# Forgetting attention: last keys in an idle ring, head 0's loads ahead of a store, later heads' loads tied to the release of their tiles

## The chip, the cores and the metric

The kernel runs on one core of one Trainium2 chip. Its engines are TensorE (PE in the profile; PEld is its weight load), VectorE (DVE), ScalarE (ACT), GpSimd (POOL) and SyncE (SP), which only issues transfers. The metric is the device time of one execution in microseconds. All data are float32; a float32 product is made of three matmuls over a high and a low part of each operand.

## The reference, cut to what matters

The reference is one residual block over 1024 tokens of width 1024: a norm, one projection into three token mixers, their merge with sigmoid gates, an output projection, and a gated feed-forward part. The change touches the second mixer, forgetting attention, with 8 heads of width 64:

```python
qh = _rmsnorm(q.reshape(B, T, FOX_HEADS, FOX_DH), q_g).transpose(0, 2, 1, 3)
kh = _rmsnorm(k.reshape(B, T, FOX_HEADS, FOX_DH), k_g).transpose(0, 2, 1, 3)
log_f = jax.nn.log_sigmoid(f_logit + f_bias)
Fc = jnp.cumsum(log_f, axis=1).transpose(0, 2, 1)
for blk in range(T // Q_BLOCK):                    # 8 blocks of 128 queries
    lo, hi = blk * Q_BLOCK, (blk + 1) * Q_BLOCK
    s = (jnp.einsum('bhqd,bhkd->bhqk', qh[:, :, lo:hi], kh[:, :, :hi]) * scale
         + Fc[:, :, lo:hi, None] - Fc[:, :, None, :hi])
    p = jax.nn.softmax(jnp.where(mask, s, -jnp.inf), axis=-1)
    outs.append(jnp.einsum('bhqk,bhkd->bhqd', p, vh[:, :, :hi]))
```

The first mixer is a gated recurrence; its decay needs the logarithm and the running sum of a projected gate, per head.

## The kernel before, in words

The program is written in stages, and a list scheduler, which works on estimated durations, sets the order of the instructions on each engine. Priorities (`high_priority`) and `issue_after` (this instruction is not placed ahead of that one) steer it. On the chip each engine then runs its own list strictly in order and waits by semaphores. SP's transfers use eight semaphores in turn, so each issue also waits until the transfer eight places ahead has landed.

**Projections with tokens as rows** (`stage`, `tm_unit`). The last of these stages, `stage(4, put_fqk(1))`, makes the normed keys and queries of heads 4 to 7. `put_fqk` appends two steps, `keys(0)` and `keys(1)`, for each quarter of the product: four transposes on TensorE into PSUM, a cast to the high part on ACT (line 628), the low part on DVE (line 629), both into a tile `ko`, and one SP store of 512 KB into the DRAM tensor `kqd` of the head pair (line 639). `ko` is a ring of two tiles, so a cast has to await the landing of the store two before. The ring `ws` beside it, of two tiles as large, holds sums of weights in these stages. The last quarter is c = 1, n = 0 of head pairs 2 and 3.

**The fill** (`fill_steps`, `cm_unit`). The remaining projections, for the recurrence and the gates, are units of seven products of Strassen's kind; their matmuls are the rows with `pp<-B11h,uh`, `T2h`, `T3h` and so on. A unit loads four tiles `ur` of weights (SP, line 802), makes sums `us` on POOL, casts `uh` on ACT, the remainder `ul` on DVE. A result goes into a tile `uo` (a ring of two) and to the DRAM tensor `hgd` of its head of the recurrence, from SP (line 789) or, for the gate, from POOL (line 782). In between, `decays(h)` loads the stored gate into one tile `fk` (SP, line 950), works on it on DVE (953, 954), takes its logarithm on ACT (956), scans (959, 960), and stores it.

**The attention** (`fox_attn`, woven with the fill head by head, and ahead of it in priority). `fox_load` fetches for a head: `kh`, `qa`, `kl`, each in two halves of 256 KB, one pair of tiles for even heads and one for odd; the cumulated gate `nf`, 2 x 256 KB; the values `vhl`, 512 KB. Lines 1030 and 1031 are the logits, first qa with kh, then qa with kl, into a PSUM ring `lg` of two. DVE adds the bias and takes the maximum (line 1036; the diagonal's bias `nfm` comes from POOL), ACT exponentiates (1046), POOL divides (1048), TensorE transposes (1059 to 1062) and multiplies with the values into the single PSUM bank `po` (1071, 1072). `yp` (ACT copy 1075, DVE sum 1076) empties that bank, and SP stores it into `yd` (1077), four stores a head. In this kernel the loads of every head but the first are tied to `marks["head"]`, the first of the four `yd` stores of the head before. The tiles of the attention lie where the rings `ko`, `ws` and others of the projections lay, and await their release.

Of the kernel before, what the change touches and what calls it, by code (L numbers as in the profile page):

```python
# [9 lines left out]
F32 = mybir.dt.float32  # L10
F32R = mybir.dt.float32r
# [4 lines left out]
P = 128  # L16
# [3 lines left out]
HB = 512  # L20
# [13 lines left out]
AHEAD = 300  # L34
# [35 lines left out]
def tile_block(ctx: ExitStack, tc: tile.TileContext, xT, x_rows, memT, vec, fbias, mats, hmask, w_ff, w_tm, w_cm,  # L70
               w_mkv, w_br, w_out, w_up, w_dn, outT):
    nc = tc.nc
    V, S, G, PE, SP = nc.vector, nc.scalar, nc.gpsimd, nc.tensor, nc.sync
# [33 lines left out]
    def col(i):  # L107
        return cv[:, i:i + 1]
# [47 lines left out]
    negFd = tc.dram_tile([8, T], F32, name="negFd")  # L156
    kqd = [tc.dram_tile([2, P, 2, T], F32, name=f"kqd{p}") for p in range(4)]
    vhd = [tc.dram_tile([P, 8, 4, P], F32, name=f"vhd{c}") for c in range(2)]
# [20 lines left out]
    def ws_tile(name="ws", dt=F32):  # L179
        return rp.tile([P, T], dt, tag="ws", name=name, bufs=2)  # L180
# [7 lines left out]
    def ko_tile(name="ko", dt=F32R):  # L188
        return rp.tile([P, 2, HB], dt, tag="ko", name=name, bufs=2)
# [430 lines left out]
    def turned(z, what, gc, tiles, ptr):  # L620

        for b in range(4):
            PE.transpose(ptr[:, b * P:(b + 1) * P], z[:, b, what * P:(what + 1) * P], ident)
        h, l = tiles
        if gc is None:
            split(S, h, l, ptr)
            return
        S.activation(h, ptr, AF.Copy, scale=gc)
        V.scalar_tensor_tensor(out=l, in0=ptr, scalar=gc, in1=h.bitcast(F32), op0=ALU.mult, op1=ALU.subtract)

    def put_fqk(pp):
        def put(c, n, z, bank):
            p = 2 * pp + c
            head_norm(z, 4, bank)

            def keys(what):
                t = ko_tile()
                turned(z, what, col(C_FK) if what == 0 else fqs, (t[:, 0, :], t[:, 1, :]), bank[what])
                SP.dma_start(kqd[p][what][:, :, n * HB:(n + 1) * HB], t.bitcast(F32))
            pending.append(lambda: keys(0))  # L640
            pending.append(lambda: keys(1))
        return put
# [89 lines left out]
    marks = {}  # L732
# [27 lines left out]
    def put_gate(i):  # L760
# [7 lines left out]
            S.dma_start(gd[i, n], t)  # L768
        return put

    def put_hg(what, h):
        def put(c, n, ps, e):
            t = out_tile()
            dst = hgd[h][what][:, n * HB:(n + 1) * HB]
            if what == 0:
                if e is None:
                    S.activation(t, ps, AF.Tanh, scale=-0.5)
                else:
                    combine(t, ps, e, c)
                    S.activation(t, t, AF.Tanh, scale=0.5)  # L780
                G.tensor_scalar(t, t, TMIN, TMAX, ALU.max, ALU.min)
                G.dma_start(dst, t)
                return
            else:
                z = e if e is not None else ur.tile([P, HB], F32, tag="ue", name="ue", bufs=3)
                combine(z, ps, e, c)
                S.activation(t, z, AF.Tanh, scale=0.5)
                V.scalar_tensor_tensor(out=t, in0=t, scalar=1.0, in1=z, op0=ALU.add, op1=ALU.mult)
            SP.dma_start(dst, t)
        return put  # L790

    def cm_unit(u, puts):
# [197 lines left out]
    resets = pf.tile([P, 256], F32, tag="resets", name="resets")  # L990
    SP.dma_start(resets, mats[:, 3 * P:3 * P + 256])
    mskf = pf.tile([P, P], F32, tag="mskf", name="mskf")
    with tc.high_priority(2 * AHEAD):
        SP.dma_start(mskf, mats[:, 2 * P:3 * P])

    def fox_load(h):
        p, a = h // 2, slice(64 * (h % 2), 64 * (h % 2) + 64)
        kh, qa, kl = (pf.tile([P, T], F32R, tag=f"{t}{h % 2}", name=f"{t}_{h}") for t in ("kh", "qa", "kl"))
        for t, (u, v) in ((kh, (0, 0)), (qa, (2, 3)), (kl, (1, 1))):
            SP.dma_start(t[0:64, :].bitcast(F32), kqd[p][u // 2][a, u % 2, :])  # L1000
            SP.dma_start(t[64:128, :].bitcast(F32), kqd[p][v // 2][a, v % 2, :])
        nf = [pf.tile([P, HB], F32, tag="nf", name="nf", bufs=3) for _ in range(2)]
        for n, t in enumerate(nf):
            SP.dma_start(t, negFd[h:h + 1, n * HB:(n + 1) * HB].partition_broadcast(P))
        vhl = pf.tile([P, 8, P], F32R, tag="vhl", name="vhl", bufs=2)
        SP.dma_start(vhl.bitcast(F32), vhd[h // 4][:, :, h % 4, :])
        return kh, kl, qa, vhl, nf

    begun = marks["product"]

    def fox_attn(h):
        p, a = h // 2, slice(64 * (h % 2), 64 * (h % 2) + 64)
        with tc.issue_after(marks["head"].ins) if h else nullcontext():
            kh, kl, qa, vhl, nf = fox_load(h)
        for tp in range(4):
            pts = []
            for j in range(2):
# [59 lines left out]
            stored = SP.dma_start(yd3[1][a, p, tp * 256:(tp + 1) * 256], yp)  # L1077
            if tp == 0:
                marks["head"] = stored
            yield  # L1080

    for h in range(8):
# [479 lines left out]
    for p in range(NF // 2):  # L1562
# [41 lines left out]
        for i in range(2):  # L1604
            f = 2 * p + i
            c = pq.tile([P, T], F32, tag="fc", name="fc", bufs=4)
# [89 lines left out]
    for a, b, own, first, c, n, sign, last, xq in (  # L1696
# [6 lines left out]
        dst = banks if own else ybanks  # L1703
# [130 lines left out]
```

## Time and profile before

| what | value |
|---|---|
| median of 3 runs (lowest, highest) | 1690.49 us (1685.17, 1690.71) |
| the profiled execution | 1690.35 us, its span 1688.6 us |
| attention heads in the span | first logits at 333.6 us, first logits of kh in the last head up to 669.7 us |
| TensorE busy | 98% of the span |
| DVE, ACT, POOL busy | 72%, 50%, 27% |

A row of a timeline has the start in us, the duration, the engine, the line, the operation with output and inputs, the shapes, a count where equal ones were merged, and in brackets the idle time of that engine just before, with what ended it. Rows of SPq are issues of transfers; their duration is that of the issue. A group of transfers ends with the size and the us from issue to landing.

### The profile page before, as it was taken

To read this page: it belongs to the slowest core of one execution; us is meant where nothing else is said; L and a number is where in the kernel's file an instruction comes from. 1 tells how busy PE (TensorE), PEld (TensorE's weight loads), DVE (VectorE), ACT (ScalarE), POOL (GpSimd) and SP (SyncE) were. 2 spreads that over 40 slices of the span, in tenths; PEclk is the share of its full clock that TensorE was granted. 3 is DMA by queue.
4 is the path that set the end of the run, shared out by engine and by line. 5 is a ranking of instruction groups with operands and counts; after the bars stand their busy time and mean duration, and the time that the engine had idled before them with its cause. 6 is when DMAs were issued, how large, how long until landed. Compare 5 with 4: busy or idle time off the path is not lost. (4 is left out here: it accounts for less than half of the span.)

```text
span 1688.6 us, 24989 instructions
## 1 busy us (share of the span) xinstructions
PE 1658.2 (98%) x8915; PEld 1419.6 (84%) x8915; DVE 1218.8 (72%) x2173; ACT 845.8 (50%) x1453; POOL 449.7 (27%) x475
## 2 busy tenths in 40 slices
PE   8999999999899999999999999899999999999999
PEld 6989999787788888888888788788888888888887
DVE  6775766588776766688766768877887878675664
ACT  7645554466666666556333267534444443343432
POOL 0143543556554444223001053311111110100000
PEclk9999999999999999999999999999999999999999
DMA  7352443565455552647866798856543452394782
GB/s 268 109 188 90 142 166 119 186 203 162 159 159 156 153 160 95 200 132 231 314 185 163 246 225 209 235 164 183 166 131 119 138 158 81 127 392 154 240 281 88
DMA packets 132637, 298.73 MB, mean 177 GB/s; under 512 B 14072, under 2 KB 31736, under 8 KB 131872
## 3 DMA queue, kind: packets, MB, share of 16 engines
q1 hardware_dynamic: 100864, 210.08, 36.8%
q0 software_dynamic: 22432, 72.36, 16.6%
q10 hardware_dynamic: 9216, 14.68, 2.3%
q8 instruction: 70, 1.15, 0.3%
q14 instruction: 55, 0.45, 0.1%
HBM read 216.40 MB, written 103.22 MB: 189 GB/s over the span
## 5 line engine op out<-in xcount | busy, mean ns | idle before, releaser
L1349 ACT CAST wh<-s 128x512 fp32r<-128x512 f32 x80 | 49.0, 620 | 118.9 <-PE pp L123 66.2
L128 ACT CAST dwh<-wr 128x1024 fp32r<-128x1024 f32 (+1 forms) x41 | 40.2, 981 | 114.9 <-PE tr L123 39.3
L1487 POOL DMA_DIRECT2D rw<-in_w_up x40 | 22.9, 602 | 244.4 <-DVE wl L1350 175.7
L1349 ACT CAST wh<-rw 128x512 fp32r<-128x512 f32 x70 | 42.8, 620 | 85.3 <-PE pp L123 43.3
L736 ACT CAST uh<-ur 128x512 fp32r<-128x512 f32 x78 | 48.2, 618 | 70.7 <-PE pp L123 67.4
L737 DVE TENSOR_TENSOR ul<-us,uh 128x512 fp32r<-128x512 f32 x72 | 55.2, 771 | 21.5 <-ACT uh L736 21.4
L1048 POOL TENSOR_SCALAR pt<-pt,st 128x128 f32<-128x128 f32 (+3 forms) x64 | 56.6, 885 | 52.5 <-DVE st L1047 32.8
L1046 ACT ACTIVATE pt<-pt,st 128x128 f32<-128x128 f32 (+3 forms) x64 | 49.8, 778 | 41.1 <-DVE st L1043 35.8
L136 DVE TENSOR_TENSOR dwl<-wr,dwh 128x1024 fp32r<-128x1024 f32 (+1 forms) x41 | 46.3, 1130 | 31.8 <-ACT dwh L128 31.7
L122 PE MATMUL pp<-B21h,uh 128*128 128x512 f32 x168 | 66.7, 399 | 2.2 <-DVE ue L150 1.2
L123 PE MATMUL pp<-T2l,uh 128*128 128x512 f32 x168 | 67.0, 399 | 0.0
L122 PE MATMUL pp<-T2h,uh 128*128 128x512 f32 x168 | 66.8, 401 | 0.0
L737 DVE TENSOR_TENSOR ul<-ur,uh 128x512 fp32r<-128x512 f32 x78 | 61.9, 795 | 6.5 <-ACT uh L736 6.0
L742 POOL TENSOR_TENSOR us<-ur 128x512 f32<-128x512 f32 x36 | 50.7, 1408 | 59.3 <-DMA ur<-in_w_cm 43.8
L124 PE MATMUL pp<-B21h,ul 128*128 128x512 f32 x168 | 66.2, 394 | 0.1
L124 PE MATMUL pp<-T2h,ul 128*128 128x512 f32 x168 | 66.2, 395 | 0.0
L123 PE MATMUL pp<-B21l,uh 128*128 128x512 f32 x168 | 66.0, 393 | 0.0
L736 ACT CAST uh<-us 128x512 fp32r<-128x512 f32 x72 | 43.9, 615 | 38.3 <-POOL us L742 21.9
L1350 DVE TENSOR_TENSOR wl<-rw,wh 128x512 fp32r<-128x512 f32 x70 | 47.0, 686 | 18.9 <-PE pp L124 15.3
L742 POOL TENSOR_TENSOR us<-us,ur 128x512 f32<-128x512 f32 x36 | 49.5, 1375 | 39.4 <-issue 33.8
L1024 POOL TENSOR_TENSOR nfm<-nf,mskf 128x128 f32<-128x128 f32 x64 | 37.9, 592 | 77.5 <-DVE st L1036 56.1
L136 DVE TENSOR_TENSOR wl<-raw,wh 128x1024 fp32r<-128x1024 f32 x29 | 38.1, 1323 | 25.6 <-ACT wh L128 25.3
(746 smaller groups left out, 6188.7 us busy)
## 6 DMA issues: line engine op xcount, KB each, us to landing
rw<-in_w_up POOLq DMA_DIRECT2D x40, 512.0 KB, 4.8
ur<-in_w_cm SPq DMA_DIRECT2D x72, 256.0 KB, 3.3
sd<-in_w_dn POOLq DMA_DIRECT2D x30, 512.0 KB, 8.3
br<-yd SPq DMA_DIRECT2D x30, 512.0 KB, 5.5
gd<-uo ACTq DMA_DIRECT2D x48, 256.0 KB, 3.1
gt<-gd SPq DMA_DIRECT2D x48, 256.0 KB, 4.5
yd<-fc SPq DMA_DIRECT2D x44, 256.0 KB, 2.8
raw<-in_w_tm SPq DMA_DIRECT2D x20, 512.0 KB, 3.5
```

The costliest lines, as they stand in the source:

```text
L122: PE.matmul(ps, lh, rh, start=first, stop=False, skip_group_check=more)
L123: PE.matmul(ps, lh, rl, start=False, stop=False, skip_group_check=more)
L124: return PE.matmul(ps, ll, rh, start=False, stop=last, skip_group_check=more)
L128: S.copy(out, in_)
L136: return (sub or V).tensor_sub(l, src, h.bitcast(F32))
L736: marks["cast"] = S.copy(h, src)
L737: V.tensor_sub(l, src, h.bitcast(F32))
L742: G.tensor_add(t, a, b)
L1046: S.activation(pt[:, :ns], pt[:, :ns], AF.Exp, bias=st[:, 2:3], accum_out=st[:, 3:4])
L1048: G.tensor_scalar(pt[:, :ns], pt[:, :ns], st[:, 3:4], 0.0, ALU.mult, ALU.add)
L1349: late["cast"] = S.copy(h, src)
L1350: late["split"] = V.tensor_sub(l, src, h.bitcast(F32))
```

## The change

1. The last two key tiles (pair 3, second half; written `(pp, c, n) == (1, 1, 0)`) are taken from the ring `ws` and no longer from `ko`.
2. The store of the second half of the query gate q of the recurrence's head 0 (`put_hg(1, 0)`, n = 1) is held back and issued only behind head 0's six key and query loads; these get the higher priority, with the mask `mskf` that had it alone.
3. Head 1's six loads are tied to that store, those of head h from 2 on to the last `yd` store of head h - 2, whose tiles they reuse. `nf` stays behind the first `yd` store of the head before, `vhl` goes behind the six loads.

```diff
             def keys(what):
                 t = ko_tile()
+                if (pp, c, n) == (1, 1, 0):
+                    t = ws_tile("ko", F32R).rearrange("p (a b) -> p a b", a=2)
...
-            SP.dma_start(dst, t)
+            if (what, h, n) == (1, 0, 1):
+                put_late.append(partial(SP.dma_start, dst, t))
+            else:
+                marks["stored"] = SP.dma_start(dst, t)
...
-    with tc.high_priority(2 * AHEAD):
-        SP.dma_start(mskf, mats[:, 2 * P:3 * P])
...
-        for t, (u, v) in ((kh, (0, 0)), (qa, (2, 3)), (kl, (1, 1))):
-            SP.dma_start(t[0:64, :].bitcast(F32), kqd[p][u // 2][a, u % 2, :])
-            SP.dma_start(t[64:128, :].bitcast(F32), kqd[p][v // 2][a, v % 2, :])
+        before = ends.get(h - 2) or marks["stored"] if h else None
+        with tc.issue_after(before.ins) if before else tc.high_priority(2 * AHEAD):
+            for t, (u, v) in ((kh, (0, 0)), (qa, (2, 3)), (kl, (1, 1))):
+                SP.dma_start(t[0:64, :].bitcast(F32), kqd[p][u // 2][a, u % 2, :])
+                loaded = SP.dma_start(t[64:128, :].bitcast(F32), kqd[p][v // 2][a, v % 2, :])
+        if not h:
+            with tc.high_priority(2 * AHEAD):
+                SP.dma_start(mskf, mats[:, 2 * P:3 * P])
+            with tc.issue_after(loaded.ins):
+                marks["stored"] = put_late.pop()()
         nf = [pf.tile([P, HB], F32, tag="nf", name="nf", bufs=3) for _ in range(2)]
-        for n, t in enumerate(nf):
-            SP.dma_start(t, negFd[h:h + 1, n * HB:(n + 1) * HB].partition_broadcast(P))
+        with tc.issue_after(marks["head"].ins) if h else nullcontext():
+            for n, t in enumerate(nf):
+                SP.dma_start(t, negFd[h:h + 1, n * HB:(n + 1) * HB].partition_broadcast(P))
         vhl = pf.tile([P, 8, P], F32R, tag="vhl", name="vhl", bufs=2)
-        SP.dma_start(vhl.bitcast(F32), vhd[h // 4][:, :, h % 4, :])
+        with tc.issue_after(loaded.ins):
+            SP.dma_start(vhl.bitcast(F32), vhd[h // 4][:, :, h % 4, :])
...
-        with tc.issue_after(marks["head"].ins) if h else nullcontext():
-            kh, kl, qa, vhl, nf = fox_load(h)
+        kh, kl, qa, vhl, nf = fox_load(h)
...
+            ends[h] = stored
```

Since the scheduler starts over with these ties, the order moves on all engines from here to the middle of the merge of the branches. Three places of it follow. Line numbers of the changed kernel are 2 to 15 higher: 1006 and 1007 are its loads of kh, qa and kl, 1012 the store held back, 809 ur, 1044 and 1045 the logits.

First, SP between the last key stores and head 0's loads, before:

```order
L639 DMA kqd_96<-ko 256x1x512
L802 DMA ur<-in_w_cm 128x512
L639 DMA kqd_96<-ko 256x1x512
L789 DMA hgd_101<-uo 128x512
L994 DMA mskf<-in_mats 128x128
L1000 DMA kh_3815<-kqd_93 64x1024
L1001 DMA kh_3815<-kqd_93 64x1024
L1000 DMA qa_3816<-kqd_93 64x1024
L1001 DMA qa_3816<-kqd_93 64x1024
L1000 DMA kl_3817<-kqd_93 64x1024
L1001 DMA kl_3817<-kqd_93 64x1024
```

and now, on to head 1's loads (kh_4151, qa_4152):

```order
L641 DMA kqd_96<-ko 256x1x512 x2
L809 DMA ur<-in_w_cm 128x512
L1006 DMA kh_3815<-kqd_93 64x1024
L1010 DMA mskf<-in_mats 128x128
L1007 DMA kh_3815<-kqd_93 64x1024
L1006 DMA qa_3816<-kqd_93 64x1024
L1007 DMA qa_3816<-kqd_93 64x1024
L1006 DMA kl_3817<-kqd_93 64x1024
L1007 DMA kl_3817<-kqd_93 64x1024
L1012 DMA hgd_101<-uo 128x512
```

```order
L796 DMA hgd_101<-uo 128x512
L1006 DMA kh_4151<-kqd_93 64x1024
L1007 DMA kh_4151<-kqd_93 64x1024
L1006 DMA qa_4152<-kqd_93 64x1024
L1007 DMA qa_4152<-kqd_93 64x1024
L1006 DMA kl_4153<-kqd_93 64x1024
L1007 DMA kl_4153<-kqd_93 64x1024
L1019 DMA vhl<-vhd_97 128x8x128
L796 DMA hgd_101<-uo 128x512
L957 DMA fk_4262<-hgd_101 128x1024
L809 DMA ur<-in_w_cm 128x512 x4
```

The two last key stores moved together, the fill's store of hgd moved behind head 0's loads, and seven loads of head 1 moved ahead of the decay's load and the next unit's weights.

Second, TensorE around the low part of head 0's first two logits, before:

```order
L122 MATMUL pp<-T2h,uh 128x512
L123 MATMUL pp<-T2l,uh 128x512
L124 MATMUL pp<-T2h,ul 128x512
L124 MATMUL pp<-T1h,ul 128x512
L1031 MATMUL lg<-kl_3817,qa_3816 128x128
L1031 MATMUL lg<-kl_3817,qa_3816 128x256
```

and now:

```order
L1044 MATMUL lg<-kh_3815,qa_3816 128x128
L1044 MATMUL lg<-kh_3815,qa_3816 128x256
L1045 MATMUL lg<-kl_3817,qa_3816 128x128
L1045 MATMUL lg<-kl_3817,qa_3816 128x256
L122 MATMUL pp<-T1h,uh 128x512
L123 MATMUL pp<-T1l,uh 128x512
```

The products with kl moved up past 15 matmuls of the fill, to right behind those with kh.

Third, DVE at the decays' tile of the recurrence's last head (fk_6499 before, fk_6501 now; before, a `yp` stood right behind it), before:

```order
L1036 ISA pt,st<-lg,nf 128x512
L1036 ISA st 128x1
L953 TENSOR_SCALAR fk_6499<-fk_6499,nc_71,c1p 128x1024
L1076 TENSOR_TENSOR yp<-po,yp 64x256
L1036 ISA pt,st<-lg,nf 128x128
```

and now, where that `yp` stands 19 rows ahead:

```order
L739 TENSOR_TENSOR ul<-ur,uh 128x512
L1055 TENSOR_TENSOR st<-st 128x1
L960 TENSOR_SCALAR fk_6501<-fk_6501,nc_71,c1p 128x1024
L1057 TENSOR_SCALAR st<-st 128x1
L961 TENSOR_SCALAR fk_6501<-fk_6501,c_70,c_69 128x1024
L1090 TENSOR_TENSOR yp<-po,yp 64x256
L148 SCALAR_TENSOR_TENSOR ue<-pp,ue 128x512
```

The first decay operation moved behind one `yp` and now has the next `yp` three rows behind it.

More of the change, by code (lines that the diff above doesn't have):

```diff
@@ L769, in put_gate @@
         return put
+    put_late = []
     def put_hg(what, h):
@@ L998, in fox_load @@
         kh, qa, kl = (pf.tile([P, T], F32R, tag=f"{t}{h % 2}", name=f"{t}_{h}") for t in ("kh", "qa", "kl"))
-        for t, (u, v) in ((kh, (0, 0)), (qa, (2, 3)), (kl, (1, 1))):
-            SP.dma_start(t[0:64, :].bitcast(F32), kqd[p][u // 2][a, u % 2, :])
-            SP.dma_start(t[64:128, :].bitcast(F32), kqd[p][v // 2][a, v % 2, :])
+        before = ends.get(h - 2) or marks["stored"] if h else None
[8 more added lines that the diff above has]
+                marks["stored"] = put_late.pop()()
         nf = [pf.tile([P, HB], F32, tag="nf", name="nf", bufs=3) for _ in range(2)]
-        for n, t in enumerate(nf):
-            SP.dma_start(t, negFd[h:h + 1, n * HB:(n + 1) * HB].partition_broadcast(P))
+        with tc.issue_after(marks["head"].ins) if h else nullcontext():
+            for n, t in enumerate(nf):
+                SP.dma_start(t, negFd[h:h + 1, n * HB:(n + 1) * HB].partition_broadcast(P))
         vhl = pf.tile([P, 8, P], F32R, tag="vhl", name="vhl", bufs=2)
-        SP.dma_start(vhl.bitcast(F32), vhd[h // 4][:, :, h % 4, :])
+        with tc.issue_after(loaded.ins):
+            SP.dma_start(vhl.bitcast(F32), vhd[h // 4][:, :, h % 4, :])
         return kh, kl, qa, vhl, nf
+    ends = {}
     begun = marks["product"]
```

## The prediction, made before the changed kernel ran

> **What bounds the kernel now.** I read the page first, for the share of TensorE, then the same busy times by stretches of the run, to see where TensorE is not busy.
>
> ```profile
> span 1688.6 us, 24989 instructions
> PE 1658.2 (98%) x8915; PEld 1419.6 (84%) x8915; DVE 1218.8 (72%) x2173; ACT 845.8 (50%) x1453; POOL 449.7 (27%) x475
> ...
> 300.00:400.00 100.00, 94.08 (x470) 77.07 (x469) 72.45 (x173) 59.06 (x106) 59.60 (x52) 0.98 0.59 195
> 400.00:420.00 20.00, 19.32 (x102) 16.17 (x101) 17.85 (x53) 11.90 (x24) 9.56 (x10) 1.00 0.55 144
> 420.00:440.00 20.00, 17.33 (x97) 14.83 (x97) 14.30 (x34) 13.56 (x23) 8.67 (x9) 1.00 0.57 201
> 440.00:460.00 20.00, 18.35 (x95) 15.20 (x94) 14.26 (x39) 11.90 (x24) 13.52 (x15) 1.00 0.38 127
> 600.00:700.00 100.00, 100.00 (x534) 85.36 (x534) 64.00 (x173) 59.01 (x118) 38.17 (x44) 1.00 0.37 117
> ```
>
> After a stretch and its length, such a row has the busy time of PE, PEld, DVE, ACT and POOL, then the granted TensorE clock, the DMA share and GB/s. TensorE bounds the kernel. Only 1688.6 - 1658.2 = 30.4 us of the span are idle on it, and 5.92 + 0.68 + 2.67 + 1.65 = 10.9 us of these lie between 300 and 460 us, where heads 0 to 2 of the forgetting attention run; in the last heads, from 600 to 700, it is full. The change can take off no matmul. It can win idle time and slow-clock time in that stretch, and lose some anywhere up to the gated sums.
>
> Next the clock in steps of 5 us, and TensorE's own waits in order of time:
>
> ```profile
> 330.00:335.00 5.00, 2.58 (x12) 1.84 (x11) 1.19 (x2) 0.17 (x1) 2.70 (x3) 0.93 1.01 246
> 335.00:340.00 5.00, 5.00 (x19) 4.05 (x18) 1.97 (x7) 2.24 (x4) 0.76 (x2) 0.73 1.13 354
> 435.00:440.00 5.00, 5.00 (x31) 4.38 (x30) 4.99 (x10) 2.71 (x4) 1.00 (x1) 1.00 0.72 261
> 460.00:465.00 5.00, 5.00 (x21) 4.12 (x20) 5.00 (x15) 4.44 (x4) 1.52 (x1) 0.66 0.89 230
> ...
> 333.61 0.47 PE L1030 MATMUL lg<-kh,qa 128*128 128x128 f32 x2 [2.42 <-DMA qa<-kqd]
> 333.92 0.40 PE L122 MATMUL pp<-T1h,uh 128*128 128x512 f32 x1
> 338.95 0.39 PE L1031 MATMUL lg<-kl,qa 128*128 128x128 f32 x2
> 351.35 0.39 PE L122 MATMUL pp<-B11h,uh 128*128 128x512 f32 x1
> 371.04 0.30 PE L1031 MATMUL lg<-kl,qa 128*128 128x128 f32 x1 [1.10 <-DMA kl<-kqd]
> 419.73 0.30 PE L1031 MATMUL lg<-kl,qa 128*128 128x128 f32 x1 [0.68 <-DMA kl<-kqd]
> 434.65 0.36 PE L1071 MATMUL po<-ph,vhl 128*128 128x256 f32 x1 [2.67 <-DVE yp L1076]
> 458.91 0.36 PE L1071 MATMUL po<-ph,vhl 128*128 128x256 f32 x1 [1.59 <-DVE yp L1076]
> ```
>
> Head 0's first logits wait 2.42 us for its loads, and the clock is low just behind: 5 x (0.07 + 0.27) = 1.7 us. The wait of 1.59 us at 458.91 is followed by 5 x 0.34 = 1.7 us of the same; that of 2.67 us at 434.65 is not. Of the waits, those of 2.42, 1.10 and 0.68 are ended by a head's loads, those of 2.67 and 1.59 by DVE.
>
> [...]
>
> **Part 1: the last keys and head 0's loads.** SP, ACT and DVE ahead of the first logits, and landing times of those transfers:
>
> ```profile
> 314.17 1.28 DVE L737 TENSOR_TENSOR ul<-us,uh 128x512 fp32r<-128x512 f32 x2
> 317.00 0.69 ACT L628 ACTIVATE ko<-lg,cv 128x512 fp32r<-128x512 f32 x1 [2.84 <-PE pp L124]
> 317.72 0.75 DVE L629 SCALAR_TENSOR_TENSOR ko<-lg,cv,ko 128x512 fp32r<-128x512 f32 x1 [2.28 <-ACT ko L628]
> 321.05 0.69 ACT L628 ACTIVATE ko<-lg,fqs 128x512 fp32r<-128x512 f32 x1 [2.36 <-DMA kqd<-ko]
> 315.60 0.64 SPq L802 DMA_DIRECT2D ur<-in_w_cm  x1
> 322.55 0.52 SPq L639 DMA_DIRECT2D kqd<-ko  x1
> 325.39 0.52 SPq L1000 DMA_DIRECT2D kh<-kqd  x1
> 327.58 0.45 SPq L1001 DMA_DIRECT2D qa<-kqd  x1
> 328.73 0.58 SPq L1001 DMA_DIRECT2D kl<-kqd  x1
> ...
> kqd<-ko SPq DMA_DIRECT2D x1, 512.0 KB, 4.9
> kqd<-ko SPq DMA_DIRECT2D x1, 512.0 KB, 6.1
> qa<-kqd SPq DMA_DIRECT2D x1, 256.0 KB, 5.9
> hgd<-uo POOLq DMA_DIRECT2D x1, 256.0 KB, 7.2
> DMA to landing us min/median/max: 6.1/6.2/6.6
> ...
> 315.00:320.00 5.00, 5.00 (x24) 4.12 (x23) 1.79 (x3) 1.68 (x3) 0.76 (x1) 1.00 1.00 352
> ```
>
> The first four of the landing rows end with the us from issue to landing; the row of min/median/max is kl's.
>
> In the other ring both casts run without waiting for a key tile: ACT is free at 317.00 - 2.84 = 314.2 and ends them at 315.6; DVE is free at 314.17 + 1.28 = 315.45, two parts of 0.75 end at 316.2 and 317.0; SP is free at 316.2. So the last store is issued at 317.0 in place of 322.55. It doesn't come through 5.5 us earlier: DMA is full there (share 1.00 at 352 GB/s), and the other last store, 512 KB or 1.5 us, is now right ahead. I take 317.0 + 4.9 + 1.5 = 323.4; the ends are 317.0 + 4.9 and 317.0 + 6.1 + 1.5, that is 321.9 and 324.6.
>
> Head 0's first load now waits for the landing of both stores, since its tile lies in that ring's place. It thus goes at 323.4 in place of 325.39. The second half of qa followed 2.2 us later, now with mskf between (0.5): 326.1 + 5.9 = 332.0. The second half of kl followed 3.3 us later: 327.2 + 6.2 = 333.4 (from 321.9 and 324.6, with 6.1 and 6.6, 331.8 and 335.0).
>
> In the new order the kl logits stand right behind the kh logits, where there were 15 matmuls between. TensorE is out of work at 333.61 - 2.42 = 331.2 as before, and its next fill matmul comes after kl, at 333.4 + 0.2 = 333.6 in place of 333.92; the kl pair (0.3) is then done as well. Gain 0.6 us, not 2.4; ends -1.0 and 2.2. The slow clock behind it stays, as the wait is nearly as long (0; at best 1.7). The store of the fill goes behind kl, at 327.8. ACT's next use of that uo tile awaits its landing, by 335.0 with the longest time above (7.2). In the new order the casts for the next T1 and T2 products stand ahead of that use: 24 matmuls, 5.0 us as the 24 of 315 to 320, from 333.6 to 338.6. So I take 0; landing later than that, it would hold up T3's cast by as much.
>
> **Part 2: heads 1 and up.** Head 1's loads now go out right behind head 0's and not behind head 0's first yd store, head 2's behind the last yd store of head 0 and not the first of head 1. The waits 1.10 and 0.68 go: 1.8 us (at worst 0). What stands behind the seven issues pays. For head 1 that is the fill's next weights:
>
> ```profile
> 336.92 0.63 ACT L787 ACTIVATE uo<-ue 128x512 f32<-128x512 f32 x1 [6.74 <-DMA hgd<-uo]
> 337.28 1.33 SPq L802 DMA_DIRECT2D ur<-in_w_cm  x3
> 461.84 0.59 SPq L1000 DMA_DIRECT2D kl<-kqd  x1
> ```
>
> Seven issues of 0.6 put the weights at 337.28 + 4.2 = 341.5; with 6.5 us, between qa's 5.9 and POOL's 7.2, they land at 348.0, and cast and remainder (0.69 + 0.75 as the keys') end at 349.4. TensorE needs them at 351.35 less 0.6. I take 0. The upper end is 2.4: the 2.0 MB of the seven (six of 256 KB, one of 512) take 5.8 us at 352 GB/s, 1.6 more than their issues, POOL's 7.2 is 0.7 above 6.5, and the decay load that goes out between is 512 KB more, 1.5: 3.8 later, of which the slack of 350.75 - 349.4 takes 1.4.
>
> ACT's wait of 6.74 us is for a POOL-issued store that took 7.2 us while head 0's loads were in the air. [...] It speaks against this part, since 2.0 MB more join that store; with the upper end of 2.4 the sum below would be 2.3 us.
>
> **Part 3: what the new order does at head 3's loads.** DVE at 457 us:
>
> ```profile
> 457.62 0.81 DVE L953 TENSOR_SCALAR fk<-fk,nc,c1p 128x1024 f32<-128x1024 f32 x1 [2.75 <-DMA fk<-hgd]
> 458.35 0.41 DVE L1076 TENSOR_TENSOR yp<-po,yp 64x256 f32<-64x256 f32 x1
> 463.33 0.20 DVE L1043 TENSOR_SCALAR st<-st 128x1 f32<-128x1 f32 x1
> ```
>
> DVE stood 2.75 us for the decay tile fk, and yp behind it held the po bank, hence TensorE's 1.59 us. In the new order yp stands 19 rows ahead of that fk operation, the work of 458.35 to 463.33, 5.0 us. So 1.59 + 1.7 = 3.3 us go. But fk's load now stands behind head 3's seven issues, 4.2 us: DVE may wait 2.75 + 4.2 - 5.0 = 2.0 us for it later, with another yp three rows behind. I charge 1.0, half, since that yp's bank is needed later: gain 2.3 (ends 0 and 3.3).
>
> The wait of 2.67 us stays: there fk, its scans and yp follow each other as before, with one short operation more ahead of yp. The rest of the reordering I take at 0; ends 1.7 us of gain, as one slow stretch, and 5.3 us of loss, two waits like 2.67.
>
> Sum: 0.6 + 1.8 + 2.3 = 4.7 us off the profiled execution's 1690.35 (span 1688.6 and 1.75 around it), which is 0.14 below the median of the runs: about **1686 us**.
>
> **Rivals.** (a) No change, 1689 to 1693: the 2.3 of part 3 turns into a wait at the second yp, and what parts 1 and 2 win is stood off at 434.65, where the chain through fk's load, not TensorE, ends last. For it: that wait is untouched. Against: the chain begins at the fill's own products, which come earlier too. (b) A large gain, every term at its upper end: 2.2 + 1.7 + 1.8 + 3.3 + 1.7 = 10.7, so 1680, and 1677 where the 2.67 goes too. For it: that no slow clock followed the 2.67. Against: kl's landing. (c) Slower: the run of seven issues holds up the fill's weights and stores at each of heads 1 to 7. It decides from 4.7 / 7 = 0.7 us a head; at 2.0 a head it is 14 - 4.7 = 9.3, so 1700. For it: ACT's 6.74. Against: the loads stood in one run before too (461.84 is one), and TensorE is at 100.00 of 100 in 600 to 700.
>
> **Numbers.** The gain of 1682 to 1689 has 0.50, (a) 0.23, (b) 0.14, (c) 0.13, from 1693 up. 0.5% is 8.5 us, about what a measurement here can tell. Faster by that, below 1682: (b) nearly whole, 0.13. Slower, above 1698.9: half of (c), 0.07. Between: 0.80. The range 1680 to 1694 leaves out half of (b) and most of (c).
>
> **What would show it.** The last kqd store at about 317; the first kh load at 322 to 325; a wait of TensorE at the first kl logits (not kh alone), about 2 us in all, slow clock behind it; no wait at the kl logits of heads 1 and 2; no yp wait at the fk of h 3; the 2.67 us still there. The forecast is wrong if the weights of the fill come late behind loads of a head, seen as waits of POOL or ACT for ur and of TensorE at B11, or if kl lands by 331.5.

## The result, and the profile after

The changed kernel takes 1701.24 us (median of 6 runs, 1698.65 to 1703.06), the kernel before 1689.85 us beside it (6 runs, 1685.17 to 1691.16): a ratio of 1.0072, 95% interval 1.0060 to 1.0085. That is 0.7% slower, where 1686 us and a range up to 1694 had been forecast. The profiled execution has a span of 1700.8 us, 12.2 more than before's 1688.6.

Up to 300 us the two lose alike (9.6 and 10.1 us, counted as below), so the loss can be read by stretch. Three stretches, first of the kernel before and then of the changed one (columns as in the prediction: stretch, length, busy time of PE, PEld, DVE, ACT, POOL, then granted clock, DMA share, GB/s):

```profile
300.00:345.00 45.00, 42.43 (x206) 34.96 (x205) 25.55 (x51) 22.06 (x39) 23.25 (x18) 0.96 0.67 215
345.00:500.00 155.00, 146.66 (x758) 122.18 (x757) 126.27 (x335) 101.10 (x188) 89.40 (x88) 0.99 0.52 168
500.00:700.00 200.00, 200.00 (x1086) 171.49 (x1085) 133.65 (x389) 119.06 (x243) 83.67 (x99) 1.00 0.45 139
```

```profile
300.00:345.00 45.00, 41.69 (x200) 34.82 (x199) 23.88 (x50) 20.24 (x37) 23.19 (x18) 0.92 0.69 214
345.00:500.00 155.00, 142.16 (x717) 117.93 (x716) 117.45 (x320) 96.52 (x175) 78.42 (x80) 0.97 0.50 164
500.00:700.00 200.00, 200.00 (x1081) 171.07 (x1080) 130.07 (x398) 118.40 (x243) 90.16 (x104) 1.00 0.44 135
```

From here on, "lost" in a stretch means TensorE's idle time plus (1 - granted clock) times the time, both summed over rows of 5 us. Before: 4.3 us between 300 and 345, 10.0 between 345 and 500. After: 6.8 and 17.9. The 10.4 us between these make most of the 12.2, half of it idle time (5.2) and half slow clock (5.2); nothing is lost between 500 and 700 in either.

TensorE's waits in the changed kernel, in order of time:

```profile
332.54 0.47 PE L1044 MATMUL lg<-kh,qa 128*128 128x128 f32 x2 [1.84 <-DMA qa<-kqd]
334.48 0.77 PE L1045 MATMUL lg<-kl,qa 128*128 128x128 f32 x2 [1.47 <-DMA kl<-kqd]
372.98 0.36 PE L1044 MATMUL lg<-kh,qa 128*128 128x256 f32 x1 [2.37 <-DVE st L1050]
376.78 0.38 PE L1085 MATMUL po<-ph,vhl 128*128 128x256 f32 x1 [0.60 <-ACT ph L128]
379.36 0.33 PE L1073 MATMUL tr<-ident,pt 128*128 128x128 f32 x1 [2.20 <-DVE pl L136]
380.81 0.51 PE L122 MATMUL pp<-B22h,uh 128*128 128x512 f32 x1 [0.43 <-ACT ue L749]
440.74 0.38 PE L1085 MATMUL po<-ph,vhl 128*128 128x256 f32 x1 [2.90 <-ACT ph L128]
441.72 0.50 PE L122 MATMUL pp<-B22h,uh 128*128 128x512 f32 x1 [0.59 <-ACT ue L749]
480.29 0.58 PE L1085 MATMUL po<-ph,vhl 128*128 128x256 f32 x1 [2.57 <-ACT ph L128]
...
330.00:335.00 5.00, 1.69 (x8) 1.08 (x7) 1.29 (x2) 1.62 (x3) 1.96 (x3) 0.85 1.02 294
335.00:340.00 5.00, 5.00 (x13) 3.94 (x13) 3.89 (x13) 2.15 (x5) 3.46 (x5) 0.50 0.97 313
340.00:345.00 5.00, 5.00 (x23) 4.07 (x23) 2.51 (x10) 2.77 (x6) 1.73 (x3) 0.96 1.04 240
```

The waits for kl of heads 1 and 2 and the 1.59 us for yp are gone, as forecast. The 2.67 us for yp, which the forecast kept, is gone as well, with 2.90 and 0.59 us for ph and ue near its place. What is there instead of all these: a wait in two parts at the first logits, with 5 x (0.15 + 0.50 + 0.04) = 3.45 us of slow clock where before had 1.7; and three groups of waits at 371 to 381, 438 to 442 and 478 to 480, ended by DVE and ACT. The groups fall where the recurrence's decays (tile fk; the fk steps in what follows) pass. DVE at the first group, then ACT at all three:

```profile
371.33 0.81 DVE L960 TENSOR_SCALAR fk<-fk,nc,c1p 128x1024 f32<-128x1024 f32 x1 [2.38 <-DMA fk<-hgd]
372.06 0.55 DVE L1050 CUSTOM_DVE_ANT_0 pt<-lg,nf 128x384 f32<-128x384 f32 x1
376.29 2.44 DVE L966 TENSOR_TENSOR_SCAN fk<-resets,fk 128x256 f32<-128x256 f32 x4 [1.06 <-ACT fk L963]
378.64 0.66 DVE L136 TENSOR_TENSOR pl<-tr,ph 128x512 fp32r<-128x512 f32 x1
...
374.34 1.92 ACT L963 ACTIVATE fk<-fk 128x2048 f32<-128x2048 f32 x1 [2.15 <-DVE fk L961]
376.16 1.06 ACT L128 CAST ph<-tr 128x512 fp32r<-128x512 f32 x2
432.06 1.28 ACT L963 ACT_TABLE_LOAD   x1
435.33 1.92 ACT L963 ACTIVATE fk<-fk 128x2048 f32<-128x2048 f32 x1 [1.99 <-DVE fk L961]
437.27 1.28 ACT L1060 ACT_TABLE_LOAD   x1
440.10 1.07 ACT L128 CAST ph<-tr 128x512 fp32r<-128x512 f32 x2
473.97 1.28 ACT L963 ACT_TABLE_LOAD   x1
475.26 1.92 ACT L963 ACTIVATE fk<-fk 128x2048 f32<-128x2048 f32 x1
477.70 1.28 ACT L791 ACT_TABLE_LOAD   x1
479.65 1.07 ACT L128 CAST ph<-tr 128x512 fp32r<-128x512 f32 x2
```

DVE stands 2.38 us for fk's load; the pt row behind it empties the logits' PSUM, and TensorE waits 2.37 us for that. ACT stands 2.15 us for the same chain with ph behind it (0.60 us of TensorE), the scans hold pl (2.20). At 438 and 478 the logarithm and its changes of function table stand ahead of ph: 2.90 and 2.57 us. At 478 both changes count. At 438 the first is over at 433.34, and ACT then stands 1.99 us for DVE, which itself had stood 1.35 us for fk's load.

### The profile page after: what moved, and what is told of

Same layout as the page of the kernel before. It is cut to its first block, busy times and chain, and to the rows that moved or that the text cites. A ratio compares the mean times of both kernels' runs of the same rounds, so it can differ in the third digit from the quotient of the medians.

```text
span 1700.8 us, 24994 instructions
## 1 busy us (share of the span) xinstructions
PE 1663.2 (98%) x8915; PEld 1422.4 (84%) x8915; DVE 1208.7 (71%) x2173; ACT 844.4 (50%) x1453; POOL 447.4 (26%) x475
## 5 line engine op out<-in xcount | busy, mean ns | idle before, releaser
L1050 DVE CUSTOM_DVE_ANT_0 pt<-lg,nf 128x512 f32<-128x512 f32 (+2 forms) x80 | 41.5, 523 | 25.3 <-PE tr L1073 15.3
L1038 POOL TENSOR_TENSOR nfm<-nf,mskf 128x128 f32<-128x128 f32 x64 | 34.4, 537 | 87.3 <-DVE st L1050 73.8
```

What stands on the lines that cost most here:

```text
L1050: V.tensor_tensor_reduce(out=pt[:, s0 + lo:s0 + hi], in0=ps[:, lo:hi], in1=bias, op0=ALU.add, op1=ALU.max, scale=1.0, scalar=-3e38, accum_ ...
```

## The experiments

What each kernel lost, in us, by the profiled execution, and its ratio to the kernel before, run beside it:

| kernel | median us | ratio (95%) | 300-345 | 345-500 | 500-700 | 700-1100 |
|---|---|---|---|---|---|---|
| before; again (one execution) | 1689.85; 1689.16 | 1 | 4.3; 1.9 | 10.0; 9.6 | 0; 0 | 8.9; 9.0 |
| changed; again (one execution) | 1701.24; 1700.53 | 1.0072 (1.0060-1.0085) | 6.8; 6.9 | 17.9; 16.4 | 0; 0 | 10.5; 13.2 |
| 1 ring alone | 1696.13 | 1.0028 (1.0015-1.0042) | 6.8 | 12.4 | 0 | 8.2 |
| 2 late store alone | 1688.30 | 0.9989 (0.9976-1.0002) | 3.7 | 9.7 | 0 | 10.4 |
| 3 early loads alone | 1693.13 | 1.0007 (0.9991-1.0023) | 2.5 | 12.8 | 0.6 | 13.4 |
| 4 changed, no early loads | 1699.21 | 1.0051 (1.0033-1.0070) | 7.1 | 15.7 | 0 | 8.8 |
| 5 before, fk later | 1680.06 | 0.9946 (0.9932-0.9960) | 1.6 | 0 | 3.6 | 7.6 |
| 6 changed, fk later | 1695.96 | 1.0037 (1.0022-1.0051) | 7.6 | 1.3 | 7.2 | 14.8 |
| 7 changed, no table loads | 1698.14 | 1.0053 (1.0041-1.0065) | 7.5 | 12.2 | 0 | 10.8 |
| 8 changed, no ring | 1693.21 | 1.0025 (1.0014-1.0037) | 3.4 | 6.5 | 0 | 11.6 |
| 9 changed, kl back | 1692.85 | 1.0027 (1.0013-1.0040) | 3.2 | 9.0 | 0.4 | 12.1 |
| 10 before, reordered | 1691.10 | 1.0020 (1.0006-1.0035) | 2.1 | 10.1 | 0 | 10.0 |
| 11 before, reordered | 1693.01 | 1.0022 (1.0009-1.0036) | 1.6 | 10.0 | 0 | 10.0 |
| 12 no ring, fk later | 1692.36 | 1.0026 (1.0011-1.0041) | 5.4 | 2.3 | 5.0 | 8.3 |
| 13 ring alone, kl back | 1697.40 | 1.0050 (1.0032-1.0068) | 2.1 | 11.5 | 0.9 | 9.5 |
| 14 changed, kl back, fk later | 1690.70 | 1.0015 (0.9999-1.0030) | 8.1 | 1.1 | 5.1 | 10.2 |
| 15 before, kl forward | 1695.14 | 1.0039 (1.0025-1.0052) | 7.5 | 9.1 | 0 | 13.1 |
| 16 late store, fk later | 1683.52 | 0.9961 (0.9945-0.9977) | 3.4 | 0 | 1.9 | 14.5 |

The columns are of one execution each. One execution can lie 4.8 us off its kernel's median (run 16: 1688.27), so sums of columns hold to no better than that. Those of runs 8, 12 and 13 lie 3.5 to 4.4 us below their medians, so their columns show too little of the loss. The median of the kernel before, run beside them, went from 1687.96 us (runs 13 to 16) to 1691.71 (runs 1 to 4); kernels of different groups therefore compare by their ratios.

**Do the readings repeat?** Second profiles of both unaltered kernels.

> The changed kernel unaltered, for a second profile. If the losses by stretch belong to its order, the waits for st, pl and ph at the fk steps come again in the same rows: 6 to 7.5 us of idle and slow clock between 300 and 345 us, 15 to 19 between 345 and 500. If they belong to the execution that was profiled: another distribution, with 345 to 500 at 12 or less.

> The kernel before unaltered, for a second profile. If the losses belong to its order: 2 to 4.5 us between 300 and 345 us, 8 to 12 between 345 and 500. If to the execution: outside of these.

Those of the changed kernel, then of the kernel before:

```profile
300.00:345.00 45.00, 41.55 (x194) 34.41 (x193) 24.29 (x54) 20.48 (x40) 23.11 (x21) 0.92 0.73 227
345.00:500.00 155.00, 143.74 (x723) 118.74 (x722) 121.43 (x319) 97.65 (x176) 80.39 (x81) 0.97 0.49 161
```

```profile
300.00:345.00 45.00, 43.09 (x215) 35.45 (x214) 25.35 (x50) 23.05 (x39) 23.33 (x18) 1.00 0.67 219
345.00:500.00 155.00, 145.36 (x758) 120.06 (x756) 128.23 (x338) 100.77 (x189) 88.81 (x87) 1.00 0.51 167
```

The difference over both stretches is 10.4 us in the first pair and 11.8 in the second, on a difference of the medians of 11.4. The loss belongs to the order, and to these two stretches; 1.9 us at the first logits of the kernel before is just under the 2 to 4.5 expected. The slow clock of the kernel before does not repeat, 3.4 us in the first pair's two stretches and none in the second; that of the changed kernel does, 8.6 and 8.5.

**Which part sets it off?** Each part alone, and the whole without one.

Run 1, ring alone:

```diff
                 t = ko_tile()
+                if (pp, c, n) == (1, 1, 0):
+                    t = ws_tile("ko", F32R).rearrange("p (a b) -> p a b", a=2)
```

> The kernel before with the last two key tiles in the idle ring and nothing else of the change. Theory A (the loss is made by the early loads of heads 1 to 7, which put the recurrence's fk steps in front of the attention's softmax casts on VectorE and ScalarE): the fk loads stay ahead of the heads' loads, so no new wait for ph or pl at an fk step; 1687 to 1692 us, within 3 us of before. Theory B (any reordering by the scheduler does it; the ring moves the last key stage, and the instruction orders behind it differ from before in two thirds of the PE rows): 1696 to 1701 us, with waits of 2 to 3 us for ph or pl behind Ln. Theory C (the first logits alone): at most 1693 us, with the loss inside 320 to 345 us.

Run 2, the late store and head 0's higher priority alone, the other heads' loads as before:

```diff
+            if (what, h, n) == (1, 0, 1):
+                put_late.append(partial(SP.dma_start, dst, t))
...
+            with tc.issue_after(loaded.ins):
+                marks["stored"] = put_late.pop()()
```

> The kernel before with head 0's six loads and the mask ahead of one store of the fill, and nothing else of the change. Theory A: the stores of the last keys still set the first load, so the first logits come no earlier; the later hgd store moves the first fk load by about 5 us and with it the first fk step; 1689 to 1694 us. Theory B (any reordering): 1696 to 1701 us. Theory D (the order at the first head makes the 2.65 us that after lost between 320 and 345 us): 1692 to 1694 us, all of it in that stretch.

Run 3, early loads alone:

```diff
+        before = ends.get(h - 2) or marks["stored"] if h else None
+        with tc.issue_after(before.ins) if before else nullcontext():
+            for t, (u, v) in ((kh, (0, 0)), (qa, (2, 3)), (kl, (1, 1))):
```

> The kernel before with the loads of heads 1 to 7 behind the last store of the head two before (head 1 behind the fill's store), and nothing else of the change. Theory A: the two waits for kl go (1.8 us), and the fk steps of recurrence heads 1 to 3 are served late and hold up the casts: some 5 us more of PE waits between 360 and 485 us and three slow stretches of 1.7 us; 1695 to 1700 us, and no loss at 320 to 345 us. Theory B': the early loads are harmless or gain and the ring does the harm: 1686 to 1690 us. Rival of the prediction (seven issues in a row hold up the fill's weights): waits of PE for DMA ur or for casts of ur, at each head alike, 1700 us.

Run 4, the change without early loads:

```diff
-        before = ends.get(h - 2) or marks["stored"] if h else None
+        before = marks["head"] if h else None
```

> The changed kernel with the loads of heads 1 to 7 where they were before (behind the first store of the head before); ring and late store stay. Theory A: what is left is the loss at the first logits, 2.65 us: 1691 to 1694 us, with the waits for kl of heads 1 and 2 back. Theory B (reordering, set off by the ring): still 1697 to 1702 us, with waits for ph or pl behind an fk step.

Run 8, the change without the ring:

```diff
-                if (pp, c, n) == (1, 1, 0):
-                    t = ws_tile("ko", F32R).rearrange("p (a b) -> p a b", a=2)
```

> The changed kernel with the last two key tiles back in the ring ko; late store and early loads stay. Three kernels with the ring wait 1.5 to 1.9 us at the first kl logits and have 3.4 us of slow clock, three without it don't wait there. Theory A' (the ring loses 2.5 us at the first logits and the other parts add about -1 and +3 at most, by their single runs): 1688 to 1694 us, no wait at the first kl logits. Rival (early loads and late store together make the loss): 1697 to 1701 us.

Theory A, the early loads, fell: alone they are within the noise (1.0007), and without them the change still loses 0.51%. Ring alone costs 0.28%, ring and late store 0.51%, all three 0.72%; late store and early loads without the ring 0.25%. So the ring is in every combination of parts that costs more than 0.28%, but it is not the only part that can cost: 0.28% for it and 0.25% for the other two together are not told apart. The parts don't add: alone they come to 0.24%, and late store, which costs nothing alone, stands at 0.51% with the ring (the intervals of this and of ring alone overlap a little). Ring with early loads, without the late store, was not run. Run 2's time lies just below all of its theories, run 3's between its two. All kernels with the ring and with kl where the change put it wait 0.7 to 1.9 us at the first kl logits, with 3.4 to 3.5 us of slow clock.

**The place of kl.** Run 9 ties the kl matmuls of the first two logits of head 0 behind the fill's T2 product, so that 14 matmuls lie between again; run 13 does that with the ring alone; run 15 does the reverse to the kernel before, which has no ring. (In runs 9, 13 and 14 the fill's counts per head begin with 0, 4, 5 in place of 2, 6, 5, as four steps are written ahead of the heads.)

```diff
+    run_all(islice(fill, 4))
+    marks["t2"] = marks["product"]
...
+                    with tc.issue_after(marks["t2"].ins) if h == 0 and tb < 2 else nullcontext():
                         PE.matmul(ps[:, :w], qa[:, tsl], kl[:, s0:s0 + w], start=False, stop=True)
```

> The changed kernel with the kl matmuls of head 0's first two logits tied behind the fill's T2 product, so that 14 fill matmuls stand between the kh and the kl logits again, as before the change; ring, late store and early loads stay. Theory A' (the ring's loss at the first logits is that kl was planned where it can't have landed): the wait at kl (1.5 to 1.9 us) goes, and the slow clock behind it (3.4) falls to 1.7 or less: 2.5 to 3.5 us less between 300 and 345 us, and the rest as in the changed kernel, 1697 to 1699 us. Rival (the later start itself sets off the waits between 345 and 500 us, since the plan ran ahead of the chip): those shrink too, 1688 to 1693 us. Third: the loss is the wait for qa, and moves there: 1700 to 1702 us.

> Ring alone, with the kl matmuls of head 0's first two logits tied behind the fill's T2 product. Ring alone took 1696.1 us, with 6.8 us lost between 300 and 345 us and 12.4 between 345 and 500. Theory A'' (the kl matmuls planned too early are the ring's whole harm, at the first logits and in what follows): 3 to 4.5 us between 300 and 345, 9 to 10.5 after it, 1688 to 1692 us. Rival (the tie helped the full change by another accident of the order): no more than the first logits' 3 us, 1693 us or above.

```diff
+            with tc.issue_after(marks["kl0"].ins) if marks.get("kl0") and b in ("T1", "T2") else nullcontext():
                 marks["product"] = mm3(...)
...
+                    low = PE.matmul(ps[:, :w], qa[:, tsl], kl[:, s0:s0 + w], start=False, stop=True)
+                    if h == 0 and tb == 1:
+                        marks["kl0"] = low
```

> The kernel before, with nothing of the change, but the fill's T2 and T1 products tied behind the kl matmuls of head 0's first two logits, so that these stand right behind the kh ones as in the changed kernel; the scheduler knows here that the loads land late. Place of the rows alone: the wait at kl (1.5 to 1.9 us) and the long slow clock (3.4) come without the ring: 6 to 8 us lost between 300 and 345 us, 10 as before between 345 and 500: 1691 to 1694 us. If lateness at the first logits carries on into the fk steps: 12 to 16 us there, 1695 to 1700 us. If the ring itself is what loses: no change, 1688 to 1691 us.

The tie takes the changed kernel from a ratio of 1.0072 to 1.0027 (1692.85 us): 3.6 us less are lost between 300 and 345, 8.9 less between 345 and 500, and the time is where the rival had it. Run 15 brings the wait about without any ring; its rows of TensorE:

```profile
330.48 0.46 PE L1031 MATMUL lg<-kh,qa 128*128 128x128 f32 x2 [1.53 <-DMA qa<-kqd]
333.45 0.77 PE L1032 MATMUL lg<-kl,qa 128*128 128x128 f32 x2 [2.50 <-DMA kl<-kqd]
...
330.00:335.00 5.00, 2.01 (x7) 1.69 (x8) 0.00 (x0) 0.62 (x2) 1.45 (x2) 0.76 1.04 308
335.00:340.00 5.00, 5.00 (x15) 3.91 (x14) 2.66 (x10) 1.58 (x5) 0.92 (x2) 0.56 1.01 353
```

So the early rows of kl cost 3 to 5 us at the first logits, with the ring or without: runs 9 and 13 take it away, run 15 brings it. Most of that is slow clock. The idle time of the changed kernel and of run 9 there is the same (3.3 and 3.2 us, in run 9 mostly a wait of 2.60 for st), the slow clock 3.5 and 0; all seven profiles with the early rows have 3.4 to 3.5 us of it, the thirteen others 0 to 3.2. (In run 14, tied too, other waits came in their place, 1.92 us for qa and 3.04 for st.) But run 15 loses 9.1 us between 345 and 500, like before, though its time, 1695.14, lies above the first theory's 1691 to 1694 and just within the second's: being late at the first logits does not by itself carry on. And run 13 clears the first logits (2.1 us) and does not come down (ratio 1.0050, ring alone 1.0028), as its rival had it. What the tie saved in run 9 behind 345 us thus more likely came from the new order that it set off than from the earlier start; each of these has one profile.

**Is any new order that costly?** Runs 10 and 11 leave the kernel before as it is and deal the fill's steps to the heads as 3, 5, 5, ... and as 2, 5, 6, 5, ...

> The kernel before, with nothing of the change, but the fill's steps dealt to the heads as 3, 5, 5 and so on in place of 2, 6, 5: the scheduler then orders some 1600 of the PE rows otherwise from head 0 on, and no transfer, tile or operation differs. Theory B (where the fk steps fall among the attention's rows is settled by accident of the order, and any new order may cost or gain several us between 345 and 500 us): that stretch, 10.0 us of idle and slow clock before, comes out anywhere from 6 to 18, the time 1686 to 1698 us. Theory that an order in itself is neutral and only the change's transfers cost: 9 to 11 us in that stretch, 1688 to 1691 us.

> The same with the fill's steps dealt as 2, 5, 6, 5 and so on: some 1500 PE rows differ, from head 1 on. Theory B: again anywhere from 6 to 18 us lost between 345 and 500 us, and not the same as in the other reordering; 1686 to 1698 us. Neutral order: 9 to 11 us there, 1688 to 1691 us.

Between 345 and 500 us both lose what before loses, 10.1 and 10.0, as the neutral order had it; theory B's 6 to 18 holds these too, but its "not the same" fell. The times are 0.20 and 0.22% up all the same, 1691.10 and 1693.01 us and so above the neutral 1688 to 1691, the size of runs 8 and 9; the profiles don't show where.

**The fk steps.** Runs 5, 6 take them out of the units, into heads 3 to 6, behind the last yd store of the head before; runs 12, 14 and 16 do it to other combinations.

```diff
-                if u in (1, 2, 4, 5):
-                    if i == 2:
-                        steps = decays((1, 2, 4, 5).index(u))
-                    if i in (2, 4, 6):
-                        next(steps, None)
...
+        with tc.issue_after(marks["end"].ins):
             SP.dma_start(fk[:, 0, :], hgd[h][0])
...
-        weave((ahead(fox_attn(h), AHEAD), FOX_STEPS), (islice(fill, FOX_FILL[h]), FOX_FILL[h]))
+        weave((ahead(fox_attn(h), AHEAD), FOX_STEPS), (islice(fill, FOX_FILL[h]), FOX_FILL[h]),
+              *([(decays(h - 3), 3)] if 3 <= h < 7 else []))
```

> The kernel before with the four fk steps (load, DVE operations, Ln, scans, stores) taken out of the units of the fill and tied to the last yd store of heads 2 to 5, so that they fall into 500 to 690 us, where TensorE had no idle time. Theory F (what is lost between 345 and 500 us is the fk steps standing ahead of the attention's work on DVE and ACT): before's own waits at fk (1.20, 0.75, 2.67, 1.59 and one slow stretch of 1.7, in all 7.9 us) go, and the kl waits stay: 1682 to 1685 us. Theory B (any order loses about as much in 345 to 500 us): 1688 to 1693 us.

> The changed kernel with its fk steps moved in the same way. Theory F: after's waits at fk (2.37, 0.60, 2.20, 0.43; 2.90, 0.59; 2.57, and three slow stretches of 1.7 us, in all 16.8) go; what stays over the kernel before with the same move is the first logits' 2.5 us: 1684 to 1688 us, so the gap between the two kernels shrinks from 11.5 to 2 to 4 us. Theory B (order in general): the gap to that kernel stays 8 to 12 us, 1692 us or more.

> Late store and early loads without the ring, and the fk steps tied to the last yd stores of heads 2 to 5: meant to beat both kernels. If the parts add: 1680.1 (fk later alone) and the two waits for kl that the early loads take away, which were already gone there: 1678 to 1682 us. If early loads cost by themselves what their single run showed (+3.7 us up to 1100 us): 1682 to 1686 us.

> The changed kernel with both: kl tied behind T2, and the fk steps tied to the last yd stores of heads 2 to 5. Without the kl tie this took 1696.0 us, the kernel before with the fk steps moved 1680.1. Theory A'' (the kl rows are what separates the two): 1680 to 1685 us, and less than 4 us lost between 500 and 700 us. Rival (early loads cost in 500 to 700 us whatever the first logits do, as in the kernel without the ring, which lost 5.0 there): 1688 to 1693 us.

> The kernel before with the fk steps tied to the last yd stores of heads 2 to 5, and head 0's loads ahead of the fill's store; no ring, no early loads: meant to beat both kernels. If the parts add (-9.6 and -1.9 to +0.3 us): 1678 to 1681 us. If the new order costs what early loads did with it (1692.4): 1688 us or more.

The stretches 345 to 500 and 500 to 700, of run 5 and then of run 6:

```profile
345.00:500.00 155.00, 155.00 (x828) 132.25 (x827) 120.44 (x335) 97.11 (x191) 86.34 (x93) 1.00 0.52 160
500.00:700.00 200.00, 198.06 (x1051) 168.79 (x1050) 140.63 (x388) 127.89 (x240) 88.75 (x93) 0.99 0.47 149
```

```profile
345.00:500.00 155.00, 153.67 (x825) 130.93 (x824) 118.24 (x329) 94.04 (x188) 85.68 (x92) 1.00 0.48 147
500.00:700.00 200.00, 194.55 (x1021) 164.51 (x1020) 138.91 (x391) 126.22 (x239) 83.23 (x93) 0.99 0.46 151
```

In all five kernels 0 to 2.3 us are lost between 345 and 500, where the thirteen others lose 6.5 to 17.9: the fk steps are the place of that loss, in the kernel before as well. Run 5 is 9.6 us faster than the kernel before (0.9946) and the fastest of all. Run 6, however, came out where theory B had it (1692 us or more), and the gap between runs 5 and 6 is no 2 to 4 us but 15.9, more than the 11.4 between the two kernels. So the fk steps are a place where both lose time, but taking them away does not take away what makes the changed kernel slower. The profiles have 6.0 of the gap at the first logits, then 1.3, 3.6 and 7.2. The three with early loads lose 5.0 to 7.2 us between 500 and 700, the two without 3.6 and 1.9, so fk steps and early loads still get in each other's way there. Run 14 came out at 1690.7, by its rival. Run 12, meant to beat both kernels, took 1692.4 where its two sums had 1678 to 1686, no faster than the same kernel with its fk steps in the units (run 8, 1.0025 and 1.0026). Run 16 at 1683.5 lies between its two theories and did not beat run 5. The move was worth 9.6 us in the kernel before, and less in every other kernel here.

Run 7 keeps the changed kernel's order row for row and takes away the 8 changes of the table:

```diff
-            S.activation(fk, fk, AF.Ln)
+            S.activation(fk, fk, AF.Tanh, scale=-1.0)
```

> The changed kernel with Tanh (scale -1) in place of Ln in the fk steps, so that the function tables need not be changed: 8 table loads of 1.28 us go, and the order of all engines stays otherwise row for row. The decay's logarithm is not computed. Theory F with ACT as the place: the chains that end at ph (376.78, 440.74, 480.29) get 2.6 us shorter each, so 5 to 8 us of waits and up to three slow stretches go: 1690 to 1696 us. If the late landing of fk's load is the place instead: DVE's waits of 1.1 to 2.4 us remain and hold the same rows: 1698 to 1701 us.

1698.14 us, a ratio of 1.0053 in place of 1.0072, 3.1 us less: at the lower end of the second theory, with signs of both. DVE's waits for fk's load go from 2.38, 1.35 and 2.35 to 1.14, 1.39 and 1.53. The waits for ph at 441 and 480 become waits for yp and ul (2.74 and 1.33 us), that for st near 373 falls from 2.37 to 0.99, and the 2.20 for pl stays. The table loads are a part; that the rest is fk's load and the scans in line with the attention fits these waits, but no run isolated it.

## Why the prediction was wrong, step by step

- **Part 1, keys and head 0's loads: forecast 0.6 us gain (ends -1.0 and 2.2), measured 2.5 lost.** The last store did move, but its landing was mis-sized:

```profile
L641 SPq DMA_DIRECT2D kqd<-ko x2: 999/1054/1108, 316.5 to 317.7; - x2
DMA to landing us min/median/max: 7.2/7.2/7.2
324.98 0.52 SPq L1006 DMA_DIRECT2D kh<-kqd  x1
```

  Head 0's first load, which waited for these stores, went at 324.98, not 323.4 (ends 321.9 and 324.6). The last store left at 317.7, not 317.0, and took 7.2 us to land, where the forecast had 4.9 + 1.5 = 6.4. So it left 4.9 us sooner than before, the load 0.41. With it qa ended its wait at 332.54 (forecast 332.0) and kl at 334.48 (333.4), so TensorE's fill went on at 335.04 in place of 333.92. And "the slow clock stays" failed: two waits of 1.84 and 1.47 us had twice the slow clock of one of 2.42. The forecast did name the place: kl right behind kh.
- **Part 2, early loads: 1.8 us gain at heads 1 and 2.** Right as a local step: no wait for kl there, and none of TensorE for the fill's weights behind the seven issues (ACT has one, 2.20 us at 350.46). Alone the part gained nothing (run 3); its profile lost 12.8 us between 345 and 500 where before lost 10.0.
- **Part 3: 2.3 us gain forecast, 1.0 lost.** The 1.59 us and its slow clock are gone. DVE did stand some 2.0 us ahead of fk (2.35 before 471.06; fk's load, issued at 463.22, took 7.8 us to land), but the charge of 1.0 was put on yp; the wait came through ACT, where logarithm and table loads stand ahead of ph: 2.57 us and 1.7 of slow clock.
- **"The wait of 2.67 us stays."** It became 2.90 + 0.59 with 1.7 us of slow clock (granted clock 0.78 and 0.88 in the two 5 us from 440), 2.5 us more.
- **"The rest of the reordering I take at 0", ends 1.7 and -5.3. This term failed most.** It put at nothing, without a reason, what the new order does at the second fk steps. There 2.37 + 0.60 + 2.20 + 0.43 + 1.7 = 7.3 us came up (the 1.7 is a granted clock of 0.66 from 380 to 385) where the kernel before has 1.20 + 0.75:

```profile
385.89 0.47 PE L122 MATMUL pp<-B21h,uh 128*128 128x512 f32 x1 [1.20 <-DVE ue L150]
390.54 0.33 PE L1059 MATMUL tr<-ident,pt 128*128 128x128 f32 x1 [0.75 <-DVE pl L136]
```

  That is 5.4 us more, the whole lower end of this term at one place, and the prediction did not look at it. The terms as measured, -2.5 + 1.8 - 1.0 - 2.5 - 5.4 = -9.6, make most of the 10.4 us lost in the two stretches.
- **Rivals.** (c), slower at 1700, had the sign and the size but another mechanism: no run of seven issues held up the fill (run 3, run 4). That slow clock could cost as much as the waits was in no rival.

On the clock, the rows. A slow stretch of 1.7 us (5 x 0.34) followed 1.59 us of idle time in the kernel before, and none followed its 2.67. A wait of 2.60 us was followed by none in run 9 and by one in run 12. The slow stretches between 300 and 500 us last 3.41 us at a clock of 0.50 in the kernel before (two) and in the changed kernel (three, and one of 6.83). In rows of 3.41 us, the kernel before at its waits of 2.67 and 1.59 us, then run 9, then run 12:

```profile
429.87:433.28 3.41, 2.11 (x10) 1.42 (x8) 2.02 (x4) 3.36 (x5) 0.78 (x1) 1.00 0.05 17
433.28:436.70 3.42, 2.05 (x10) 1.75 (x11) 3.42 (x9) 2.75 (x4) 0.00 (x0) 1.00 0.45 172
457.18:460.59 3.41, 1.76 (x8) 1.35 (x8) 2.97 (x9) 1.45 (x3) 0.46 (x1) 1.00 0.59 216
460.59:464.00 3.41, 3.41 (x12) 2.67 (x11) 3.41 (x12) 3.39 (x3) 0.52 (x1) 0.50 0.94 251
...
339.61 0.45 PE L1044 MATMUL lg<-kh,qa 128*128 128x384 f32 x1 [2.60 <-DVE st L1051]
334.34:337.75 3.41, 2.67 (x13) 1.90 (x11) 0.07 (x1) 0.36 (x1) 1.70 (x2) 1.00 1.03 297
337.75:341.17 3.42, 1.56 (x7) 1.39 (x8) 2.79 (x11) 2.27 (x6) 1.06 (x2) 1.00 1.13 264
341.17:344.58 3.41, 3.41 (x18) 2.77 (x18) 2.03 (x11) 2.67 (x7) 2.23 (x5) 1.00 1.11 310
...
338.63 0.68 PE L1038 MATMUL lg<-kh,qa 128*128 128x384 f32 x1 [2.60 <-DVE st L1044]
335.26:338.67 3.41, 0.81 (x5) 0.35 (x3) 2.71 (x7) 2.14 (x4) 0.02 (x1) 1.00 0.61 206
338.67:342.09 3.42, 3.42 (x9) 2.87 (x10) 2.75 (x15) 2.09 (x6) 2.26 (x5) 0.50 1.02 242
```

The 2.67 us are split over two rows with 1.30 and 1.37 us of idle time, run 9's 2.60 over two with 0.74 and 1.86: the clock behind is 1.00. The 1.59 lies in one row with 1.65 us idle, run 12's 2.60 in one: clock 0.50 in the row behind. At these four waits the length alone thus did not tell what a wait cost; what did is not shown. The loss of 1.7 us is 3.41 us at a clock of 0.50.

On the table loads, the rows above have 1.28 us each, and ACT's next operation right behind (437.27 + 1.28 to the next start at 438.57): the gap is 0.02 us. Run 7's 8 switches were worth 3.1 us in all.

**What stays open.** Why the ring's order puts the fk steps so badly was not isolated: the kernels with ring and untied kl lose 12.2 to 17.9 us between 345 and 500 with the fk steps in the units, all others 6.5 to 12.8. It fits that the scheduler took the last stores to land earlier than they do and so planned the attention ahead of the chip, but run 13 speaks against that as the whole story, and no run held the order and moved the landing alone. Nor is it known where reorderings like runs 10 and 11 lose their 0.2%.

## What to carry to other kernels

When a change makes a scheduler start over, the order that comes out is itself a term of the sum: walk all places where another chain (here a load, a logarithm with its table, scans) stands in line ahead of what TensorE waits for, and price each, rather than take the remainder at 0. Price the landing and not the issue: here the last store left 4.9 us sooner, at a DMA share of 1.01 (358 GB/s from 315 to 320 us), and the load that awaited it went 0.41 us sooner, while the new order had already pulled the consumers of kl forward. And look for the chain that is in the way in both versions: moving the fk steps to a later stretch won 9.6 us in the kernel before, more than any part of the change was meant to, though with parts of the change in place the move won less.

## What was unexpected of the hardware

Two waits of 1.84 and 1.47 us, 0.5 us of work apart, were followed by 3.45 us of slow clock, more than the waits themselves. A wait of 2.60 us was followed by no slow clock in run 9, and by 1.7 us of it in run 12. And the executions of one kernel spread widely: the early loads alone ran from 1688.03 to 1698.36 us over 12 runs, the late store alone from 1686.28 to 1692.51, the kernel before beside them from 1686.21 to 1698.11 over 30, so that a single execution could not have told +0.07% from +0.5%.
